# Six small reorderings in a two-block transformer kernel: a DVE scalar moved, buffers added and moved, priorities raised, the key tile before the query tile

## The chip, the cores and the metric

The kernel runs on one core of a Trainium2 chip. The time is device time of one execution in microseconds (us). PE is the matrix engine (TensorE), PEld its weight loads, DVE the vector engine, ACT the scalar engine, POOL is GpSimd, and SP issues most of the DMAs.

## The reference

Two transformer blocks on 512 tokens of width 1024, in float32.

```
first block:   mods = silu(c) @ w_mod + b_mod            (shift, scale, gate; for c and for c_ctx)
               px = (rms(x)*g*(1+sc1)+sh1) @ w_in         (the same for 256 context tokens)
               og = gated linear attention, both ways;  od = differential attention
               x  = x + gt1 * (concat(og, od) @ w_out)
               x  = x + gt2 * swiglu(rms(x)*g*(1+sc2)+sh2)
second block:  x  = x + rms(mixer(rms(x)))                (pooling, and forget-gate attention, 8 heads)
               x  = x + rms(memory_attention(rms(x), mem))(4 heads, 256 memory tokens)
               x  = x + rms(conv_ffn(rms(x)))
```

## The kernel before, in words

Activations lie feature-major: 8 tiles of 128 features by 512 tokens. Each float32 product is made of three matmuls: a matrix is split into a high part (rounded by ACT, line 187) and a low part (a subtraction, line 188), and lines 196 to 198 multiply high by high, low by high and high by low. A weight block of 128 by 1024 comes by DMA into one of two `wf` buffers and is split into one of three `whi`/`wlo` pairs (`wsplit`), or into a buffer that the caller lends (`keep`). `fm` runs over output tiles `m` and, for each, over the 8 (or 22) input tiles `k`; with `HALVES` it does all its `m` for the first 256 tokens and then for the second 256. In a fixed number of places per tile it calls `step()`, which takes one step of a generator in `between`: that is how a norm of the stage before is spread over the matmuls of the next one.

The instruction order of each engine is laid out at compile time. Every instruction gets the running number `tc.cur_priority`; of the instructions that are ready in the planner's own clock, the one with the lowest number goes first. `wsplit` lowers the number by `WO` = 50 for its two split instructions. `tc.issue_after(ins)` places what is traced inside it behind `ins` on its engine. At run time each engine takes its instructions in that order and waits at each for what it needs.

Places that the change touches:

- **Start** (lines 424 to 445). `normed_x` squares the 8 tiles of x in pairs: ACT squares the even one (line 432), DVE the odd one (433) and adds both (434), PE sums over the 128 features (313, four matmuls a pair). The pair's tile `t` (tag `sqt0`) has two buffers, `u` (tag `sqt1`) one. `WU` matmuls on the identity (line 488) run on PE before the first sum. Then come the first two blocks of `w_mod` (line 353), the reciprocal root (165 to 170), the modulation and the first projection.
- **`gd`** (line 1171), one DVE instruction on a 128 by 1 column of `cols`; its only reader is `diff_merge`, hundreds of us later.
- **End of the first mixer** (line 1343): three accumulators of `w_out` that were filled ahead are added into X by DVE; the next PSUM tiles take their banks. Then `norm2` for the second half of the tokens is spread over the first `w_ffn_in` tiles: after `W4` steps its sum over features runs on PE, after three more its reciprocal root is broadcast.
- **Forget-gate attention** (lines 1569 to 1601). `fox_in(m)` makes a query and a key tile for two heads. `ev_q` takes one DVE product, two ACT casts and two DVE subtractions; `ev_k` one DVE product, six ACT copies and two DVE subtractions. `fox(hp_)` needs both for its scores (1614, 1615).
- **Memory attention** (lines 1686 to 1770). The pool `xp` holds `KV` (keys and values, 8 KB a partition), `Ym` and lent weight buffers. In the second half of the tokens, `KV` is reused as `Y` in `post` (lines 1438, 1452, 1453), whose generator `after` is stepped by the tiles of `w_up`. The heads' softmax is stepped by `head_step`; after the last `w_xq` tile a loop runs the heads left to their end. Pool `hq` lives on to the end of the kernel; `xp` is closed ahead of the second FFN, whose pool `fp2` takes its place in SBUF and holds the split weights `Fhi`/`Flo` lent to the fourth to sixth `w_up` block, the tiles `z` and `early`, and the FFN's hidden tiles.

Of the kernel before, what the change touches and what calls it, by code (L numbers as in the profile page):

```python
# [10 lines left out]
F32 = mybir.dt.float32  # L11
# [3 lines left out]
ALU = mybir.AluOpType  # L15
# [4 lines left out]
KT = D // 128  # L20
S = 512
TT = S // 128
CTX = 256
MEM = 256
# [22 lines left out]
QP = (0,)  # L47
Q3 = 0
MG = 1
WU, WX, WW = 15, 1, 5  # L50
MV, W0 = (0, 1), 1
XG = 9
ML = 0
W4, W5 = 1, 1
W1, W2 = 2, 2
X2 = (0, 2, 4)
XR, DR = (1, 3, 5, 7), (1, 3, 5, 7)
# [3 lines left out]
WO = 50  # L61
# [19 lines left out]
def kernel(ctx: ExitStack, tc: tile.TileContext, a: dict, out: bass.AP, stop=None):  # L81
    nc = tc.nc
    V, G, A, T = nc.vector, nc.gpsimd, nc.scalar, nc.tensor

    def f32(ap):
        return ap.bitcast(F32)
# [20 lines left out]
    def mis(dt=F32):  # L107
        return ps.tile([128, 512], dt, tag="mis", name="mis")
# [18 lines left out]
    def col(name, i):  # L127
        o = COLS[name][0] + i
        return cols[:, o:o + 1]
# [85 lines left out]
    def drain():  # L215
        while between:
            step()
# [171 lines left out]
    with tc.tile_pool(name="st", bufs=1) as st, tc.tile_pool(name="st2", bufs=2) as st2:  # L389
# [37 lines left out]
        def normed_x(x):  # L427

            pt = mis()
            for k in range(0, KT, 2):  # L430
                t, u = (st2.tile([128, S], F32, tag=f"sqt{j}", name="sqt", bufs=2 - j) for j in range(2))
                A.activation(t, x[:, k], AF.Square)
                V.tensor_tensor(u, x[:, k + 1], x[:, k + 1], ALU.mult)
                V.tensor_tensor(u, u, t, ALU.add)
                with tc.issue_after(warm(WU if k == 0 else WX)):
                    last_warm[0] = sum_sq(pt, u, k == 0, k == KT - 2)
            yield
            rb = st.tile([128, S], F32, tag="rbx", name="rbx")
            yield bcast(rb, rms(st, pt, TT, "x"))
            for k in range(KT):  # L440
                V.tensor_tensor(x[:, k], x[:, k], rb, ALU.mult)
                if k == 1:
                    yield
            yield
# [55 lines left out]
        hid = hidden(0)  # L500
# [667 lines left out]
        mnl = mlo[:, 4:8].rearrange("p k (u t) -> p (k u) t", u=2)  # L1168

    gd = midp.tile([128, 1], F32, name="gd")  # L1170
    V.tensor_scalar(gd, col("diff_norm_g", 0), 0.8, None, ALU.mult)

    def mem_in(k):
        m = ap2.tile([128, MEM], F32, tag="mk", name="mk")
# [116 lines left out]
    sp = ctx.enter_context(tc.tile_pool(name="sp", bufs=2))  # L1291
# [31 lines left out]
    def norm2(x, y):  # L1323
        for _ in range(W4 if x else W5):
            yield
        r = fm_stats(sp, sqs[:, x:y], "n2")
        for _ in range(3 if x else 1):
            yield
        bcast(rb[:, x:y], r)
        for k in range(KT):  # L1330
            if k % 2:
                yield
            t = sp.tile([128, S // 2], F32, tag="n2t", name="n2t")
            V.tensor_tensor(t, X[k][:, x:y], rb[:, x:y], ALU.mult)
            modulated(t, h2[0][:, k, x:y], h2[1][:, k, x:y], sc2[:, k:k + 1], mods[:, 24 + k, 0:1], sp, "n2u")

    with tc.tile_pool(name="wo", bufs=1) as wo:
        keep = kept(wo, (0, 1, -1, -1, -1), 0)
        have = {(m, 0): wsplit(a["w_out"][m].rearrange("p k m -> p (k m)"), 1024, None, keep()) for m in (3, 4)}
        for m, (p, whi, wlo) in enumerate(parts):  # L1340
            mm3(p, whi[:, 896:1024], wlo[:, 896:1024], mhi[:, 7], mlo[:, 7], False, True)
        for m, (p, _, _) in enumerate(parts):
            V.scalar_tensor_tensor(X[m], p, mods[:, 16 + m, 0:1], X[m], ALU.mult, ALU.add)
        for m in range(len(parts)):
            add_sq(X[m], m, 0, S)
        fm(a["w_out"], range(3, KT), KT, lambda k: mhi[:, k], lambda k: mlo[:, k], accs, ev_out, HALVES, after=norm2,
           keep=keep, have=have)
# [86 lines left out]
    def post(Y, gname, nextg, g2, tails, spread):  # L1434


        def ev(m, x, y, p):
            V.tensor_scalar(Y(m // 2 * 2, x, y)[:, m % 2], p, col(gname, m), None, ALU.mult)
            add_sq(p, m, x, y)

        def after(x, y):
            rbp = sp.tile([128, S // 2], F32, tag="rbp", name="rbp")
            r = fm_stats(sp, sqs[:, x:y], "post")
            yield
            bcast(rbp, r)
            yield
            rb2 = rbp.rearrange("p (o t) -> p o t", o=1).to_broadcast([128, 2, S // 2])
            held = hq.tile([128, 2, S // 2], F32, tag="hld", name="hld")
            for k in range(0, KT + 2, 2):
                if k < KT:  # L1450
                    y2, x2 = Y(k, x, y), XT[k // 4][:, k % 4:k % 4 + 2, x:y]
                    V.tensor_tensor(y2, y2, rb2, ALU.mult)
                    V.tensor_tensor(x2, x2, y2, ALU.add)
                    for j in (k, k + 1):
                        A.activation(g2[0][:, j, x:y], X[j][:, x:y], AF.Copy, scale=col(nextg, j))
                    t = held if k == 0 else sp.tile([128, 2, S // 2], F32, tag="sqx", name="sqx", bufs=1)
                    A.activation(t, x2, AF.Square)
                    yield
                if k > 0:
                    for j in (k - 2, k - 1):  # L1460
                        V.scalar_tensor_tensor(g2[1][:, j, x:y], X[j][:, x:y], col(nextg, j), f32(g2[0][:, j, x:y]),
                                               ALU.mult, ALU.subtract)
                    if k > 2:
                        V.tensor_tensor(held, held, last, ALU.add)
                    yield
                if k < KT:
                    last = t

            def tail():
                pt = sums()  # L1470
                for j in range(2):
                    sum_sq(pt, held[:, j], j == 0, j == 1)
                r = rms(sp, pt, (y - x) // 128, "pre")
                if spread:
                    bcast(rb[:, x:y], r)
                return r
            tails[x] = tail
        return ev, after
# [12 lines left out]
    bhi, blo = (lambda k: g2[0][:, k]), (lambda k: g2[1][:, k])  # L1491
# [78 lines left out]
    def fox_in(m):  # L1570


        qs, ka = qkF[:, m % 2, 0], qkF[:, m % 2, 1]
        kl = fpl.tile([128, 2, S], F32R, tag="kl", name="kl", bufs=2)

        def scaled(p):
            t = ft.tile([128, 16 + S], F32, tag="u", name="qk")[:, :S]
            V.tensor_tensor(t, p, rb, ALU.mult)
            return t

        def ev_q(_, x, y, p):
            t = scaled(p)
            for e in range(2):
                own, oth = slice(64 * e, 64 * e + 64), slice(64 - 64 * e, 128 - 64 * e)
                A.copy(qs[own, e], t[own])
                V.tensor_tensor(qs[oth, e], t[own], f32(qs[own, e]), ALU.subtract)

        def ev_k(_, x, y, p):
            t = scaled(p)
            for e in range(2):  # L1590
                own, oth = slice(64 * e, 64 * e + 64), slice(64 - 64 * e, 128 - 64 * e)
                A.copy(ka[own, e], t[own])
                V.tensor_tensor(kl[own, e], t[own], f32(ka[own, e]), ALU.subtract)
                A.copy(ka[oth, e], t[own])
                A.copy(kl[oth, e], f32(kl[own, e]))
        fm(a["w_q2"], [m], KT, bhi, blo, accs, ev_q)
        fm(a["w_k2"], [m], KT, bhi, blo, accs, ev_k)
        return qs, ka, kl
    fox_ops = [fox_in(0)]

# [81 lines left out]
    hq = ctx.enter_context(tc.tile_pool(name="hq", bufs=1))  # L1682
    xa = ExitStack()
    xp = xa.enter_context(tc.tile_pool(name="xp", bufs=1))
    xt = xa.enter_context(tc.tile_pool(name="xt", bufs=2))
    KV = xp.tile([128, 8, MEM], F32, name="KV")
    KVM, VM = KV[:, 0:4], KV[:, 4:8].rearrange("p (t u) n -> p t (u n)", t=2)
    g4 = new_q()
    Ym = xp.tile([128, KT, S], F32, name="Ym")
# [5 lines left out]
    if stop == "x3":  # L1695
        return finish()
    nc.sync.dma_start(KV, kvd)
    xh = hp.tile([128, 8, S], F32R, tag="hhi", name="xh")
# [52 lines left out]
    def head_step(i):  # L1751
        if next(heads[i], heads) is heads:
            heads.pop(i)
# [5 lines left out]
    for i, seg in enumerate(HALVES):  # L1759
        fm(a["w_xq"], range(4), KT, lambda k: g4[0][:, k], lambda k: g4[1][:, k], accs, head_in, (seg,), keep=xk, have=wq,  # L1760
           every=XE, lo_eng=LQ and G)
        while heads:
            for i in range(len(heads))[::-1]:
                head_step(i)
        fm(a["w_xo"], range(KT), 4, lambda k: xh[:, k], lambda k: xh[:, 4 + k], accs, ev, (seg,),
           keep=lambda: room.pop(0) if room else ok(), have=wo, every=2, lo_eng=LO and G)
        drain()
        between.append(after(*seg))
# [5 lines left out]
    bhi, blo = (lambda k: g4[0][:, k]), (lambda k: g4[1][:, k])  # L1774
# [197 lines left out]
```

## Time and profile before

| | us |
|---|---|
| median of three runs | 1642.4 (1641.32 to 1644.54) |
| the profiled execution, its time | 1641.52 |
| its span (first to last instruction) | 1639.1 |
| PE busy within the span | 1590.6 (97%) |
| DVE, ACT, POOL busy | 948.0, 718.7, 214.1 |

The granted TensorE clock is 0.989 of full speed over the span. The profiled execution has 2.4 us outside its span.

### The profile page before, as it was taken

What the parts mean: (1) busy time and instruction counts of PE and PEld (TensorE: products, weight loads), DVE (VectorE), ACT (ScalarE), POOL (GpSimd) and SP (SyncE); (2) the same over time, 40 slices, a digit from 0 to 9 for tenths busy, and PEclk for the clock granted to TensorE, in tenths of its full rate; (3) what the DMA queues carried; (4) which work ended last, traced back from release to release, by engine and by line L of the source; (5) the groups of instructions that cost most, each with busy time, mean ns of one, the idle gap of its engine ahead of it and who ended that gap; (6) DMA issues with size and microseconds to landing.
All of it is one profiled execution on the core that took longest, in us unless ns stands there. A gap on an engine that the chain in (4) does not pass through costs nothing.

```text
span 1639.1 us, 25459 instructions
## 1 busy us (share of the span) xinstructions
PE 1590.6 (97%) x10098; PEld 1355.6 (83%) x10098; DVE 948.0 (58%) x1791; ACT 718.7 (44%) x1353; POOL 214.1 (13%) x237
## 2 busy tenths in 40 slices
PE   7999999999999999999999999999998999999997
PEld 5798977778889888888889777888988988888887
DVE  5626898788765222223335676445788777776333
ACT  3424555677645323232223565224466544444221
POOL 0300000111022122210004000122000222221001
PEclk8999999999999999999999999999999999999999
DMA  8232245332322333333332212234211233323332
GB/s 350 82 89 78 66 158 180 124 100 78 128 88 78 103 94 99 91 99 94 93 114 72 77 39 65 91 103 148 84 52 34 83 93 100 103 90 97 97 93 74
DMA packets 49046, 163.23 MB, mean 100 GB/s; under 512 B 5664, under 2 KB 11296, under 8 KB 47392
## 3 DMA queue, kind: packets, MB, share of 16 engines
q1 hardware_dynamic: 45328, 158.15, 30.4%
q10 hardware_dynamic: 3312, 3.18, 0.6%
q8 instruction: 79, 1.29, 0.3%
q0 software_dynamic: 288, 0.28, 0.1%
q14 instruction: 39, 0.32, 0.1%
HBM read 158.72 MB, written 3.15 MB: 99 GB/s over the span
## 4 chain that ended last, share of the span: by engine, by line
PE 85%; DVE 5%; ACT 3%; DMA 1%; issue 1%; POOL 0%; ACTq 0%; DVEq 0%; POOLq 0%
PE acc L197 16%; PE acc L198 16%; PE acc L196 16%; PE s L198 5%; PE s L196 5%; PE s L197 5%; PE acc L286 3%; PE acc L285 3%; PE acc L287 3%; PE mis L1147 1%; PE mis L1632 1%; DVE wlo L188 1%; PE acc L775 1%; PE s L1118 1%; DMA mk<-in_memT 1%
## 5 line engine op out<-in xcount | busy, mean ns | idle before, releaser
L187 ACT CAST whi<-wf 128x1024 fp32r<-128x1024 f32 (+4 forms) x221 | 228.6, 1034 | 422.6 <-PE acc L197 277.7
L188 DVE TENSOR_TENSOR wlo<-wf,whi 128x1024 fp32r<-128x1024 f32 (+2 forms) x183 | 222.0, 1213 | 176.2 <-ACT whi L187 172.3
L196 PE MATMUL acc<-qhi,whi 128*128 128x512 f32 (+1 forms) x640 | 239.4, 374 | 0.0
L197 PE MATMUL acc<-qlo,whi 128*128 128x512 f32 (+1 forms) x640 | 239.3, 374 | 0.0
L198 PE MATMUL acc<-qhi,wlo 128*128 128x512 f32 (+1 forms) x640 | 239.3, 374 | 0.0
L196 PEld LDWEIGHTS acc<-qhi,whi 128*128 128x128 f32 x640 | 120.8, 189 | 19.6
L197 PEld LDWEIGHTS acc<-qlo,whi 128*128 128x128 f32 x640 | 120.7, 189 | 19.7 <-issue 0.2
L198 PEld LDWEIGHTS acc<-qhi,wlo 128*128 128x128 f32 x640 | 120.7, 189 | 19.3
L196 PE MATMUL s<-qhi,whi 128*128 128x512 f32 (+1 forms) x336 | 128.3, 382 | 0.0
L198 PE MATMUL s<-qhi,wlo 128*128 128x512 f32 (+1 forms) x336 | 128.3, 382 | 0.0
L197 PE MATMUL s<-qlo,whi 128*128 128x512 f32 (+1 forms) x336 | 128.2, 382 | 0.0
L188 POOL TENSOR_TENSOR wlo<-wf,whi 128x1024 fp32r<-128x1024 f32 x38 | 91.0, 2396 | 214.3 <-ACT whi L187 214.3
L1417 DVE TENSOR_TENSOR e<-e,s 128x512 f32<-128x512 f32 (+1 forms) x22 | 14.3, 651 | 154.2 <-PE s L198 154.1
L197 PE MATMUL acc<-glo,whi 128*128 128x512 f32 (+1 forms) x208 | 74.4, 358 | 0.1
L196 PE MATMUL acc<-ghi,whi 128*128 128x512 f32 (+1 forms) x208 | 74.4, 358 | 0.0
L198 PE MATMUL acc<-ghi,wlo 128*128 128x512 f32 (+1 forms) x208 | 74.2, 357 | 0.0
L196 PEld LDWEIGHTS s<-qhi,whi 128*128 128x128 f32 x336 | 64.0, 190 | 11.9
L197 PEld LDWEIGHTS s<-qlo,whi 128*128 128x128 f32 x336 | 64.0, 190 | 11.8
L198 PEld LDWEIGHTS s<-qhi,wlo 128*128 128x128 f32 x336 | 63.9, 190 | 11.8
L197 PE MATMUL acc<-Flo,whi 128*128 128x512 f32 (+1 forms) x187 | 71.6, 383 | 0.0
L285 PE MATMUL acc<-whi,hhi 128*128 128x256 f32 (+1 forms) x224 | 67.1, 299 | 3.4 <-ACT qsq L654 2.5
L286 PE MATMUL acc<-wlo,hhi 128*128 128x256 f32 (+1 forms) x224 | 65.6, 293 | 3.3 <-DVE wlo L188 3.3
(648 smaller groups left out, 3833.4 us busy)
## 6 DMA issues: line engine op xcount, KB each, us to landing
wf<-in_w_ffn_in SPq DMA_DIRECT2D x44, 512.0 KB, 3.6
wf<-in_w_up SPq DMA_DIRECT2D x44, 512.0 KB, 3.5
wm<-in_w_mod SPq DMA_DIRECT2D x32, 512.0 KB, 3.6
wm<-in_w_mod SPq DMA_DIRECT2D x8, 1024.0 KB, 11.7
wf<-in_w_ffn_out SPq DMA_DIRECT2D x16, 512.0 KB, 3.5
wf<-in_w_g SPq DMA_DIRECT2D x16, 512.0 KB, 3.5
wf<-in_w_down SPq DMA_DIRECT2D x16, 512.0 KB, 3.5
wf<-in_w_dv SPq DMA_DIRECT2D x8, 512.0 KB, 3.7
```

The source lines that it names most:

```text
L187: A.copy(hi[:, :n], wf[:, :n])
L188: (lo_eng or V).tensor_tensor(lo[:, :n], wf[:, :n], f32(hi[:, :n]), ALU.subtract)
L196: T.matmul(o, lhi, rhi, start=start, stop=False)
L197: T.matmul(o, lhi, rlo, start=False, stop=False)
L198: ins = T.matmul(o, llo, rhi, start=False, stop=stop).ins
L285: T.matmul(o, bhi(k), whi, start=k == 0, stop=False)
L286: T.matmul(o, bhi(k), wlo, start=False, stop=False)
L287: T.matmul(o, blo(k), whi, start=False, stop=k == KT - 1)
L775: T.matmul(p[32 * j:32 * j + 32, :256], silc[:, 4 * kc + j], wf[:, j * 256:(j + 1) * 256], start=kc == 0, stop=kc == 1, skip_group_check=T ...
L1118: T.matmul(s_[:, n0:n1], QF[:, c, ts], KA[:, c, n0:n1], start=True, stop=False)
L1147: T.matmul(p[:, :128], aT[:, kt * 128:(kt + 1) * 128], v, start=kt == 0, stop=kt == NKT - 1)
L1632: T.matmul(pO[:, ts], vz[:, kt, hp_, 64 * e:64 * e + 128], pT[:, kt * 128:(kt + 1) * 128], start=kt + e == 0, stop=kt - t + e == 1, skip_g ...
```

## The change

1. `WU`, the identity matmuls ahead of the first sum, goes from 15 to 13, and `u` in `normed_x` gets a second buffer.
2. `gd` is issued behind `hid`, the last DVE instruction of the first modulation.
3. `norm2` for the second half takes two steps before its sum over features (`W4`) and two after it, where it took one and three.
4. The three additions of line 1343 get a number lower by 100.
5. The broadcast tile `rbp` of `post` shares the tag `n2t` of the same shape; `KV` moves from pool `xp` to pool `hq`.
6. `fox_in` makes the key tile first, then the query tile.
7. The loop that finishes the last heads of memory attention gets numbers lower by 100.

```diff
-WU, WX, WW = 15, 1, 5
+WU, WX, WW = 13, 1, 5
-W4, W5 = 1, 1
+W4, W5 = 2, 1
...
-                t, u = (st2.tile([128, S], F32, tag=f"sqt{j}", name="sqt", bufs=2 - j) for j in range(2))
+                t, u = (st2.tile([128, S], F32, tag=f"sqt{j}", name="sqt", bufs=2) for j in range(2))
...
-    V.tensor_scalar(gd, col("diff_norm_g", 0), 0.8, None, ALU.mult)
+    with tc.issue_after(hid):
+        V.tensor_scalar(gd, col("diff_norm_g", 0), 0.8, None, ALU.mult)
...
-        for _ in range(3 if x else 1):
+        for _ in range(2 if x else 1):
             yield
...
+            tc.cur_priority -= 2 * WO
             V.scalar_tensor_tensor(X[m], p, mods[:, 16 + m, 0:1], X[m], ALU.mult, ALU.add)
+            tc.cur_priority += 2 * WO
...
-            rbp = sp.tile([128, S // 2], F32, tag="rbp", name="rbp")
+            rbp = sp.tile([128, S // 2], F32, tag="n2t", name="rbp")
...
+        fm(a["w_k2"], [m], KT, bhi, blo, accs, ev_k)
         fm(a["w_q2"], [m], KT, bhi, blo, accs, ev_q)
-        fm(a["w_k2"], [m], KT, bhi, blo, accs, ev_k)
...
-    KV = xp.tile([128, 8, MEM], F32, name="KV")
+    KV = hq.tile([128, 8, MEM], F32, name="KV")
...
+        tc.cur_priority -= 2 * WO
         while heads:
             for i in range(len(heads))[::-1]:
                 head_step(i)
+        tc.cur_priority += 2 * WO
```

## Rows read from the trace of the kernel before

**Rows 1.** The page, busy time, share of the span and instructions of PE.

```profile
PE 1590.6 (97%) x10098; PEld 1355.6 (83%) x10098; DVE 948.0 (58%) x1791; ACT 718.7 (44%) x1353; POOL 214.1 (13%) x237
```

**Rows 2.** Windows: stretch, length, busy PE PEld DVE ACT POOL (count), PEclk, DMA, GB/s.

```profile
7.00:20.00 13.00, 8.13 (x53) 6.93 (x56) 4.60 (x10) 1.73 (x4) 0.00 (x0) 0.72 1.02 413
451.50:454.50 3.00, 1.12 (x7) 0.69 (x6) 2.36 (x3) 2.09 (x3) 0.00 (x0) 1.00 0.35 86
486.00:490.46 4.46, 2.28 (x20) 2.10 (x19) 2.88 (x6) 2.18 (x5) 0.04 (x1) 1.00 0.50 151
490.46:493.87 3.41, 3.41 (x18) 3.41 (x17) 1.70 (x4) 2.61 (x5) 0.00 (x0) 0.50 0.46 133
911.00:920.00 9.00, 6.96 (x32) 5.25 (x31) 5.52 (x10) 6.79 (x11) 0.00 (x0) 1.00 0.34 113
1202.00:1210.00 8.00, 6.08 (x38) 5.03 (x37) 7.79 (x22) 6.43 (x19) 0.00 (x0) 1.00 0.01 2
1262.00:1266.84 4.84, 0.34 (x4) 0.15 (x3) 4.79 (x12) 3.51 (x8) 0.33 (x4) 0.84 0.00 0
1266.84:1272.11 5.27, 4.81 (x21) 4.51 (x22) 5.27 (x10) 5.24 (x9) 2.02 (x4) 0.50 0.41 109
1272.11:1284.11 12.00, 12.00 (x102) 12.00 (x102) 9.96 (x21) 5.59 (x11) 2.97 (x7) 1.00 0.26 85
```

**Rows 3.** Timeline of DVE, start of the kernel: start, length, operation, idle before.

```profile
6.06 0.68 DVE L434 TENSOR_TENSOR sqt<-sqt 128x512 f32<-128x512 f32 x1
...
9.40 0.15 DVE L1171 TENSOR_SCALAR gd<-cols 128x1 f32<-128x1 f32 x1 [2.52 <-DMA cols<-in_cols]
...
15.66 0.69 DVE L433 TENSOR_TENSOR sqt<-X 128x512 f32<-128x512 f32 x1 [2.01 <-PE mis L313]
16.46 0.69 DVE L434 TENSOR_TENSOR sqt<-sqt 128x512 f32<-128x512 f32 x1
```

**Rows 4.** Timeline of ACT, start: the third and fourth square.

```profile
7.74 0.63 ACT L432 ACTIVATE sqt<-X 128x512 f32<-128x512 f32 x1 [0.79 <-DMA X<-in_xT]
11.03 0.63 ACT L432 ACTIVATE sqt<-X 128x512 f32<-128x512 f32 x1 [2.66 <-DVE sqt L434]
```

**Rows 5.** Timeline of PE, start: first and last sum, second block of w_mod.

```profile
7.17 0.98 PE L313 MATMUL mis<-ones,sqt 128*128 128x32 f32 x8
...
17.20 1.92 PE L313 MATMUL mis<-ones,sqt 128*128 128x32 f32 x8 [1.00 <-DVE sqt L434]
...
23.13 1.07 PE L353 MATMUL acc<-wm,silc 128*32 128x256 f32 x16
```

**Rows 6.** Timeline of DVE, end of the first mixer.

```profile
452.13 1.23 DVE L188 TENSOR_TENSOR wlo<-wf,whi 128x1024 fp32r<-128x1024 f32 x1 [2.92 <-ACT whi L187]
453.27 0.75 DVE L1343 SCALAR_TENSOR_TENSOR X<-acc,mods,X 128x512 f32<-128x512 f32 x1
```

**Rows 7.** Timeline of DVE, entry of the first FFN.

```profile
487.57 1.23 DVE L188 TENSOR_TENSOR wlo<-wf,whi 128x1024 fp32r<-128x1024 f32 x1 [0.34 <-ACT whi L187]
488.71 0.42 DVE L1312 TENSOR_TENSOR sqs<-sqs,sqt 128x256 f32<-128x256 f32 x1
```

**Rows 8.** Timeline of PE, first scores of forget-gate attention.

```profile
919.15 0.33 PE L1615 MATMUL s<-kl,qkF 128*128 128x128 f32 x1 [1.03 <-ACT kl L1595]
```

**Rows 9.** Timeline of DVE and of PE, last heads of memory attention.

```profile
1202.44 0.69 DVE L1453 TENSOR_TENSOR X<-X,Ym 128x512 f32<-128x512 f32 x1
...
1203.91 0.44 PE L1732 MATMUL mis<-ident,sm 128*128 128x128 f32 x2 [1.14 <-DVE sm L1723]
```

**Rows 10.** Timelines of DVE, POOL and PE, entry of the second FFN.

```profile
1265.01 0.69 DVE L1453 TENSOR_TENSOR X<-X,KV 128x512 f32<-128x512 f32 x1
...
1265.90 0.13 POOL L1787 MEMSET z<- 128x2 f32 x2 [128.62 <-DVE X L1453]
...
1266.50 1.58 POOL L1792 COPY zl<-z 128x2 f32<-128x2 f32 x2 [0.47 <-DVE z L1790]
...
1266.84 0.58 PE L196 MATMUL s<-qhi,Fhi 128*128 128x256 f32 x1 [4.50 <-ACT Fhi L187]
```

## The prediction

> **What bounds the kernel now.** I read the page first. PE is busy 97% of the span [rows 1]: 1590.6 of 1639.1 us. The change takes no matmul away but two on the identity, so what it can win lies in the 48 us in which PE is not busy, and in stretches where PE is busy at half clock. I looked for every stop of PE in its timeline, then for its releaser, then cut windows around those that an edit touches. The six windows show PE short of work for 4.87, 1.88, 2.18, 2.04, 1.92 and 4.50 us (length less busy time) [rows 2]. Three of these stretches hold or are followed by a lower clock: 0.72 in the first, and 0.50 for 3.41 us from 490.46 and for 5.27 us from 1266.84; from 1272.11 the clock is 1.00 again [rows 2]. In the last window 102 matmuls take 12.00 us, 0.118 us each; by that the 18 matmuls from 490.46 would take 2.12 and lose 1.29 us to the clock, and the 21 from 1266.84 would take 2.48 of 4.81 and lose 2.33 [rows 2]. So a stop at these two places costs about half as much again, behind it, as it shows itself. I lay no rule on when the clock falls: I only count that where the stop goes, the low stretch right behind it probably goes too.
>
> **The change part by part.** Each edit is set against its own stop.
>
> *Start: `gd`, `u`, `WU`.* DVE adds the first pair at 6.06, and its next piece of work is held 2.52 us, until 9.40, by `gd`, which waits for the DMA of `cols`; nobody needs `gd` for hundreds of us [rows 3]. Meanwhile ACT squared the third pair at 7.74, when its x landed [rows 4]. Later DVE waits 2.01 us, until 15.66, for PE's sum, because `u` has one buffer [rows 3], and ACT waits 2.66 us for DVE to free `t` [rows 4]. With `gd` behind `hid` and two `u`, a pair costs DVE L433 and L434: 0.69+0.69 and some issue, about 1.5 us [rows 3]. The x transfers are 0.52 MB a pair; at 413 GB/s [rows 2] one takes 1.27 us, so the fourth is there about 7.74+1.27 = 9.0, ahead of DVE. From 6.9 three pairs take DVE to 11.4, and the last sum starts there and not at 17.20: 5.8 us earlier [rows 5]. That sum took 1.92 us where the first took 0.98 [rows 5]; the 0.94 between may go, but PE still pauses between the sums, so I take half: 5.8+0.5 = 6.3. Lower bound: only the two named waits go, 2.52+2.01 = 4.5. Upper: all of the 0.94, and as much as 1.07 more for the first block of `w_mod`, if that ran at half clock: 7.8. Would DMA take it back? The second block of `w_mod` is used at 23.13 [rows 5], then at 16.8. Behind the third pair's landing there are 0.52 of x, 0.15 of `cols` and 2.1 MB of two blocks, 2.8 MB or 6.7 us at 413 GB/s: 14.5. It lies 2.3 us clear. The two fewer identity matmuls are 0.2 us of filler ahead of a sum that waits for DVE: 0; without that cover, 0.2 won, as each is near 0.1 us by the 0.118 above. `gd` costs DVE its 0.15 us behind `hid`, beside PE's matmuls.
>
> *X additions ahead (line 1343).* PE stands 1.88 of 3.00 us [rows 2], while DVE does a 1.23 us weight subtraction first and the first addition only at 453.27 [rows 6]. The PSUM banks come free with the additions. Put ahead, the addition starts up to 1.1 us earlier, but then the subtraction is late by up to three additions of 0.75, and PE waits for that too. 0.6 (0 to 1.1).
>
> *`W4` = 2.* PE stops 2.18 us ahead of the sum of squares [rows 2], because DVE's last addition to it starts at 488.71, behind a 1.23 us weight subtraction [rows 7]. One step later means a share of a tile's matmuls in front, about 12, 1.4 us by 0.118. It covers most of the stop. At stake are 2.18+1.29 = 3.47. What is late next: the reciprocal root has one step fewer before its broadcast, and PE comes to that about when it is ready. I leave 0.65 of stop and 0.5 there: 2.3 (0.5 to 3.5).
>
> *Key before query.* PE stands 2.04 of 9.00 us; the last of it are 1.03 before the first scores, for ACT's `kl` [rows 2, 8]. `ev_k` has six copies, `ev_q` two casts; with the key tile first the six lie under the query tile's matmuls. What is late next is `ev_q`'s product, casts and subtractions, shorter but there. 1.2 (0 to 2.0). The order of loads turns with it; the DMA share of 0.34 [rows 2] leaves room.
>
> *Last heads' steps ahead.* PE stands 1.92 of 8.00 us, 1.14 at one softmax product; DVE is busy 7.79 of the 8.00 and spends 0.69 us a tile on `post`'s additions of the layer before, in front of the softmax [rows 2, 9]. Numbers lower by 100 turn these two round; the additions are needed only later. As DVE has just 0.2 us free, work is only pushed on: 1.2 (0 to 1.9).
>
> *`KV` in `hq`.* `Fhi` and `z` lie where `KV` lay. The last reader of `KV`, a 0.69 us addition, runs at 1265.01; the `z` memset, whose idle engine had waited for it, at 1265.90; `Fhi`'s first matmul at 1266.84 after 4.50 us of waiting [rows 10]. With `KV` outside the reused space, the split of `Fhi` and the memset wait for no reader of it, and the weights have their loads early. At stake: 4.50, 0.46 more of 5.27 less 4.81, and 2.33 of clock, 7.3 in all [rows 2]. But DVE is busy 4.79 of 4.84 before and 5.27 of 5.27 behind [rows 2], and what PE needs after the three lent blocks comes from the same DVE: the X tiles, their low parts, `z`. I expect one small stop of 0.5 us and a little low clock: 6.0. Lower bound: the 4.50 us only is exchanged for another wait of about 2 on DVE: 2.5. `rbp` sharing a tag: 0, as the tag's other tiles are `norm2`'s, read long before; without that, a wait of `post` for one 0.4 us addition [rows 7].
>
> Sum of the savings: 6.3+0.6+2.3+1.2+1.2+6.0 = 17.6; lower bounds 7.5, upper 23.6. The profiled execution took 1641.52 [the table above], so 1641.5-17.6 = 1623.9; it is 0.9 below the median of 1642.4, so a median of 1624 to 1625. I say 1624.
>
> **The rivals.** 0.2%, 3.3 us, is about what a measurement of this kernel can tell from no change.
>
> (1) *DVE becomes the bound at the second FFN's entry, and part of the start is given back* (0.25). For it: the full DVE rows above. Against: in the 12 us behind, DVE is busy 9.96 [rows 2], so it recovers. Then `KV` gives 2.5 and the start, where PE runs into the reciprocal root and DMA instead, 5: 17.6-3.5-1.3 = 12.8, 1628.7. [...]
>
> (2) *More than forecast* (0.12). A stop that goes also keeps the clock up behind it and every bound lies near its upper end: start 7.5, `KV` 7.2, the rest 6.5: 21.2, 1620.3 or lower to 1618.
>
> (3) *The numbers don't do what they say* (0.10). The planner's order is made anew; the edits that lower numbers, and `W4`, win nothing as the planner places the same instructions first anyway: additions, `W4`, key and heads 0, and new small stops of 3: 6.3+6.0-3 = 9.3, 1632.2; up to 1637.
>
> (4) *Slower: the ring of split weights gets late* (0.05). There are three `whi`/`wlo` pairs and 1.23 us of DVE for each low part [rows 6, 7]. If the new order lays other DVE work in front of the subtractions throughout, PE waits at each block. A block of eight input tiles serves 24 matmuls in each half of the tokens, so PE's 10098 [rows 1] are at most 210 blocks: 17.6/210 = 0.084 us a block eats the whole gain, from 0.10 a block it is slower by over 0.2%, and at 0.15 it is 1641.5-17.6+31.5 = 1655.4. Against: PE is busy 97%, so subtractions have been ahead of it elsewhere, and no edit touches the inner loops but by number.
>
> **How the numbers follow.** Forecast 0.48, with its own range 1621 to 1627. Rivals (1) 0.25, (2) 0.12, (3) 0.10, (4) 0.05. From 1618 to 1633 I hold the forecast, (1), (2) but for its tail, and half of (3). Faster by over 0.2% (below 1639.1): all but (4) and a tail of (3): 0.93. Within: 0.03. Slower: 0.04.
>
> **What would show it.** `gd` behind `hid`, the last sum of squares of x starting near 11.4, and the second `w_mod` block near 17; no wait of 4.50 at `Fhi`, and clock 1.00 in the window behind it; the stop ahead of the first FFN's sum below 1 us with full clock; no wait for `kl` at the first scores, though perhaps one for the query; softmax products without 1.14. PE's busy time should fall by 4 to 5 us, the half-clock stretches, and the rest come out of its stops. The prediction is wrong if the stops come again a few us later for the next late operand, above all at the entry of the second FFN, or if new stops stand in the inner loops, where no edit was made.

## The result and the profile after

The changed kernel takes 1625.69 us, median of 4 runs (1623.72 to 1626.96), against 1643.06 of before beside it: ratio 0.9893, 95% interval 0.9877 to 0.9908, or 17.4 us less. The forecast was 1624, with 1618 to 1633 around it. The profiled execution took 1626.83 with a span of 1625.0, so the two traces stand 14.1 us of span apart [rows 1, and the table above them]. A ratio can differ a little from the quotient of the two medians beside it.

The sum came out; most of its terms did not. Below stand the page's row for PE, then the windows that answer to those of [rows 2] (stretch, length, busy time of PE, PEld, DVE, ACT and POOL with their counts, PEclk, DMA share, GB/s):

```profile
PE 1585.2 (98%) x10094; PEld 1350.0 (83%) x10094; DVE 949.5 (58%) x1791; ACT 718.1 (44%) x1354; POOL 211.3 (13%) x237
```

```profile
7.00:20.00 13.00, 11.35 (x80) 8.48 (x80) 6.05 (x17) 3.31 (x7) 0.00 (x0) 0.74 1.01 410
...
443.50:446.10 2.60, 0.72 (x5) 0.29 (x3) 1.89 (x2) 1.01 (x2) 0.00 (x0) 1.00 0.31 128
446.27:449.69 3.42, 3.42 (x17) 3.42 (x17) 2.52 (x3) 2.22 (x4) 0.00 (x0) 0.50 0.63 200
479.50:483.24 3.74, 2.46 (x22) 2.29 (x20) 2.72 (x5) 2.47 (x4) 0.00 (x0) 1.00 0.48 142
...
1194.00:1202.00 8.00, 6.08 (x39) 5.02 (x37) 7.78 (x22) 6.44 (x19) 0.00 (x0) 1.00 0.01 2
1250.00:1262.00 12.00, 12.00 (x100) 11.84 (x100) 10.28 (x24) 9.53 (x19) 1.85 (x5) 1.00 0.20 67
```

PE is full at the second FFN's entry at clock 1.00. At the start it stops 1.65 of 13 us where it stopped 4.87. At the additions (443.50) the stop is still 1.88, and in this execution half clock (PEclk 0.50, from 446.27) follows it, which it did not in the one of before. At the last heads (1194) PE and DVE are busy as long as before, to 0.01 us: 6.08 and 7.78 of 8.00.

PE's timeline shows the same places. Behind the additions there are three stops that before did not have (at 934.59, 982.81 and 1185.69), and one that takes the place of `Fhi`'s (1280.62):

```profile
12.63 1.61 PE L313 MATMUL mis<-ones,sqt 128*128 128x32 f32 x8
...
22.47 0.50 PE L196 MATMUL s<-hhi,whi 128*128 128x512 f32 x1 [0.86 <-ACT hhi L381]
...
122.65 0.35 PE L285 MATMUL acc<-whi,hc 128*128 128x256 f32 x1 [0.97 <-DVE v_qk L166]
...
446.10 0.39 PE L196 MATMUL acc<-mhi,kh 128*128 128x256 f32 x1 [1.88 <-DVE X L1345]
...
907.14 0.33 PE L1617 MATMUL s<-qkF 128*128 128x128 f32 x1 [0.80 <-DVE qkF L1589]
...
934.59 0.38 PE L1617 MATMUL s<-qkF 128*128 128x256 f32 x1 [0.46 <-DVE sm L1622]
...
982.81 0.39 PE L1617 MATMUL s<-qkF 128*128 128x256 f32 x1 [0.46 <-DVE sm L1622]
...
1185.69 0.70 PE L1714 MATMUL s<-KV,xq 128*128 128x256 f32 x2 [1.15 <-ACT sm L1721]
...
1196.02 0.44 PE L1735 MATMUL mis<-ident,sm 128*128 128x128 f32 x2 [1.13 <-DVE sm L1726]
...
1280.62 0.50 PE L196 MATMUL acc<-qhi,whi 128*128 128x512 f32 x1 [1.42 <-DVE z L1795]
```

The start of one instruction, taken in both traces, tells how far the changed kernel is ahead, and the difference of two neighbours what a stretch gave. Each trace is one execution; how far such stretches differ between executions is told further below.

| instruction | before | after | ahead | the stretch gave |
|---|---|---|---|---|
| PE, first product of the first projection | 26.60 | 22.47 | 4.1 | 4.1 |
| PE, first product with `hc` behind `v_qk` | 132.29 | 122.65 | 9.6 | 5.5 |
| PE, product behind the additions | 454.16 | 446.10 | 8.1 | -1.6 |
| DVE, `crow`, ahead of forget-gate attention | 905.07 | 896.10 | 9.0 | 0.9 |
| PE, softmax product of the last heads | 1203.91 | 1196.02 | 7.9 | -1.1 |
| PE, `r_post` at the end | 1631.08 | 1616.75 | 14.3 | 6.4 |

So the forecast 6.3 of the start is 9.6, of which more than half comes long after the start; where the four middle edits were to give 5.3, the kernel gives back 1.8 (-1.6, 0.9, -1.1); and `KV`'s 6.0 is 6.4.

### The profile page after: what moved, and what is told of

It is laid out like the page before. It is cut to its first block, busy times and chain, and to the rows that moved or that the text cites. A ratio compares the mean times of both kernels' runs of the same rounds, so it can differ in the third digit from the quotient of the medians.

```text
span 1625.0 us, 25446 instructions
## 1 busy us (share of the span) xinstructions
PE 1585.2 (98%) x10094; PEld 1350.0 (83%) x10094; DVE 949.5 (58%) x1791; ACT 718.1 (44%) x1354; POOL 211.3 (13%) x237
## 4 chain that ended last, share of the span: by engine, by line
PE 85%; DVE 6%; ACT 4%; DMA 3%; issue 2%; POOL 1%; SPq 0%; ACTq 0%; DVEq 0%; POOLq 0%
PE acc L197 16%; PE acc L196 16%; PE acc L198 16%; PE s L196 5%; PE s L198 5%; PE s L197 5%; PE acc L285 2%; PE acc L286 2%; PE acc L287 2%; PE mis L1635 1%; PE mis L1147 1%; DVE wlo L188 1%; ACT whi L187 1%; PE acc L775 1%; PE s L1118 1%
## 5 line engine op out<-in xcount | busy, mean ns | idle before, releaser
L187 ACT CAST whi<-wf 128x1024 fp32r<-128x1024 f32 (+4 forms) x221 | 228.6, 1034 | 420.8 <-PE acc L197 281.9
L1420 DVE TENSOR_TENSOR e<-e,s 128x512 f32<-128x512 f32 (+1 forms) x22 | 14.3, 651 | 154.0 <-PE s L198 153.8
```

The source lines that it names most:

```text
L187: A.copy(hi[:, :n], wf[:, :n])
```

## The experiments

Each builds on the kernel before, unless it says otherwise.

### The start, edit by edit

The whole start edit (13 identity matmuls, two `u`, `gd` behind `hid`):

> Before with the whole start edit (13 identity matmuls, two u, gd behind hid) and nothing else. In the profile of the changed kernel PE starts the first projection 4.1 us earlier, at 22.47, and reaches the first product of the linear attention (L285, 132.29 before) 9.6 us earlier: the stop of 2.90 us at 67.47 and the half clock behind it are gone as well. If the start edit does all of that alone, this run shows the same and is 8 to 10 us faster. The prediction's reading (6.3 us, all of it within the first 24 us) would leave the stop at 67 us where it was. The rival that another edit removes that stop gives 4 to 6 us.

1634.13 against 1644.16 us, ratio 0.9949 (0.9932 to 0.9966). The start's edits do it alone: 8.4 us by the ratio, 10 by the medians.

Only the count:

```diff
-WU, WX, WW = 15, 1, 5
+WU, WX, WW = 13, 1, 5
```

> Before with 13 in place of 15 identity matmuls and nothing else. The prediction counted this at 0 to 0.2 us: the time stays within 0.5 us of before and the stop at 67.47 stays. The rival: the count also enters the clock in which the order is laid out, the matmuls from 50 to 75 us come in another order, and with it the stop of 2.90 us and the half clock behind it go: 3 to 5 us faster, with the stops of the first 20 us as before (2.60, 1.28, 1.00).

1643.48, ratio 1.0004 (0.9992 to 1.0016). The rival falls: the laid-out order does change in some places between 50 and 75 us, but the stop there stays (2.77 us, with half clock behind it).

Only `gd`:

```diff
-    V.tensor_scalar(gd, col("diff_norm_g", 0), 0.8, None, ALU.mult)
+    with tc.issue_after(hid): V.tensor_scalar(gd, col("diff_norm_g", 0), 0.8, None, ALU.mult)
```

> Before with gd behind hid and nothing else. The prediction: the 2.52 us wait of DVE goes, the second sum starts near 8.9 in place of 11.05, and the later wait for the one u buffer stays: 2 to 2.5 us faster. Rival: the single u holds the pairs back just as long, so that all the gain needs both edits: under 0.7 us. A third way: with less idle time in the first 20 us the clock of the sums rises too, and it is 3 to 4 us.

1641.87, ratio 0.9987 (0.9975 to 1.0000): 2.1 us by the ratio, which is the forecast's figure, but the interval runs from 0 to 4.1 and doesn't rule out the rival. In the trace PE starts the first projection at 25.55, 1.05 us earlier than before. DVE's timeline says why it is less than the 2.52 us that `gd` held:

```profile
8.41 0.69 DVE L433 TENSOR_TENSOR sqt<-X 128x512 f32<-128x512 f32 x1 [1.03 <-PE mis L313]
...
11.06 0.69 DVE L433 TENSOR_TENSOR sqt<-X 128x512 f32<-128x512 f32 x1 [1.17 <-PE mis L313]
...
14.56 0.69 DVE L433 TENSOR_TENSOR sqt<-X 128x512 f32<-128x512 f32 x1 [2.01 <-PE mis L313]
```

The 2.52 us of `gd` [rows 3] are gone, and each later pair now waits for PE's sum of the pair before, 1.03, 1.17 and 2.01 us, 4.2 in all. The first of these waits, 1.03, was hidden behind `gd`'s; the other two stood in the kernel before as well.

Only the second `u`:

```diff
-                t, u = (st2.tile([128, S], F32, tag=f"sqt{j}", name="sqt", bufs=2 - j) for j in range(2))
+                t, u = (st2.tile([128, S], F32, tag=f"sqt{j}", name="sqt", bufs=2) for j in range(2))
```

> Before with a second buffer for u and nothing else; gd still stands in front of the second pair until the DMA of cols has landed. The prediction counts the wait of 2.01 us for PE's sum as gone: about 2 us faster, with the stop of 2.60 us ahead of the second sum unchanged. Rival: gd alone sets the chain, and this gives under 0.7 us.

1633.39, ratio 0.9937 (0.9921 to 0.9954): some 10 us, five times the forecast, and as much as the whole start edit. In its DVE timeline two things differ from before:

```profile
7.57 0.69 DVE L434 TENSOR_TENSOR sqt<-sqt 128x512 f32<-128x512 f32 x1
...
9.73 0.15 DVE L1171 TENSOR_SCALAR gd<-cols 128x1 f32<-128x1 f32 x1 [1.33 <-DMA cols<-in_cols]
9.81 1.29 DVE L433 TENSOR_TENSOR sqt<-X 128x512 f32<-128x512 f32 x2
11.02 1.29 DVE L434 TENSOR_TENSOR sqt<-sqt 128x512 f32<-128x512 f32 x2
...
56.11 1.29 DVE L188 TENSOR_TENSOR wlo<-wf,whi 128x1088 fp32r<-128x1088 f32 x1 [0.71 <-ACT whi L187]
57.32 3.17 DVE L424 TENSOR_TENSOR cX<-cX,rbc 128x256 f32<-128x256 f32 x8
```

With two `u`, the second pair is laid out ahead of `gd`. `gd` still holds the third pair for 1.33 us, but then two pairs go through together, and PE starts the first projection at 22.80, 3.8 us earlier than before:

```profile
22.80 0.49 PE L196 MATMUL s<-hhi,whi 128*128 128x512 f32 x1 [0.86 <-ACT hhi L381]
```

And 45 us later the second low part of `w_gv` (56.11) stands ahead of the context's eight products. In the kernel before it stands behind them and behind the eight subtractions that take turns with POOL, and PE stands for it, with half clock after. DVE, PE and the window behind, of before:

```profile
68.70 0.43 DVE L383 TENSOR_TENSOR hc<-mc,hc 128x256 fp32r<-128x256 f32 x1 [0.38 <-POOL mc L382]
69.04 1.28 DVE L188 TENSOR_TENSOR wlo<-wf,whi 128x1088 fp32r<-128x1088 f32 x1
```

```profile
70.38 0.41 PE L286 MATMUL acc<-wlo,hhi 128*128 128x272 f32 x1 [2.90 <-DVE wlo L188]
```

```profile
70.62:74.03 3.41, 3.41 (x17) 3.41 (x17) 2.54 (x6) 2.12 (x5) 0.00 (x0) 0.50 0.51 163
```

To tell this order from the start itself, one run moves the split and leaves `u` single:

```diff
-        affine(scc, "norm1_g", 8, 1)
+        affine(scc, "norm1_g", 8, 1); get = tm_load(a["w_gv"], 0, 272)
         for k in range(KT):
             modulated(cX[:, k], ...
...
-    get = tm_load(a["w_gv"], 0, 272)
     for t in range(2, 6):
```

> Before with one thing moved: the first w_gv block's loads and splits are written ahead of the modulation of the context tokens, so that DVE makes the second low part ahead of the context's eight products and not behind its last eight subtractions. u has one buffer as before, and the stops of the first 20 us are to stay. Theory: the second u won about 4.6 us not at the start but by turning this order; then the stop of 2.90 us before L286 and the half clock behind it (1.7 us) go, and this run is 4 to 4.6 us faster. The rival: the stop went because PE came to it at another time, and with the order alone turned PE stops at the same place for the context's rows instead: under 1 us.

1639.13 against 1644.01, ratio 0.9970 (0.9957 to 0.9983), 4.9 us. DVE makes the low part between the products, and PE's window has no stop and full clock:

```profile
60.49 2.64 DVE L424 TENSOR_TENSOR cX<-cX,rbc 128x256 f32<-128x256 f32 x7 [1.21 <-ACT rbc L333]
63.05 1.48 DVE L188 TENSOR_TENSOR wlo<-wf,whi 128x1088 fp32r<-128x1088 f32 x1
```

```profile
66.00:74.00 8.00, 8.00 (x66) 8.00 (x65) 6.66 (x14) 4.58 (x11) 3.70 (x5) 1.00 0.26 92
```

From the start of the first projection to the first product with `hc` behind `v_qk` it is 99.6 us in this trace, 99.5 to 100.8 in the six traces with two `u`, and 102.9 to 105.8 in the seven others. So the order gives the second stretch by itself; by time it is about half of the second `u`'s gain.

### The other edits, one at a time

`KV` in `hq`, with the shared tag of `rbp`:

> Before with KV in pool hq, and rbp sharing the tag n2t, and nothing else. The prediction: 6.0 us faster (2.5 to 7.3): no wait of 4.50 us at Fhi, no half clock behind it, one small stop of about 0.5 us left. Its rival: DVE is the bound there and PE stops at z or at the low parts instead, 2.5 us faster.

1636.57 against 1643.78, ratio 0.9955 (0.9939 to 0.9970), 7.4 us. There is no wait at `Fhi`, and a stop of 1.41 us at `z` some 26 us on, as in the whole change:

```profile
1293.13 0.50 PE L196 MATMUL acc<-qhi,whi 128*128 128x512 f32 x1 [1.41 <-DVE z L1790]
```

`W4 = 2`, with two steps behind the sum:

> Before with two steps ahead of the sum of squares and two behind it, and nothing else. The prediction: 2.3 us faster, the stop of 2.18 us down to 0.65 and 0.5 left in front of the broadcast or in the clock. The profile of the changed kernel shows a stop of 1.28 there, none at the broadcast and no half clock, which would be 0.90 + 1.29 = 2.2. A rival: the half clock behind the stop stays, and it is 0.9.

1642.24, ratio 0.9994 (0.9980 to 1.0007): not to be told from no change by time. In its trace the stop ahead of the sum is 1.39 us, with no half clock behind it.

The key tile first:

> Before with the key tile ahead of the query tile and nothing else. The prediction: 1.2 us faster, the three stops of 2.04 us around the first scores falling to 0.8. A rival, from the profile of the changed kernel: it is this edit that brings new stops of 0.46 us at the later scores (934 and 982 us) and one of 1.15 us in memory attention (1184.55, where the split of a late weight stands ahead of a softmax on ACT); then it gives 0 or loses up to 1 us.

1643.39, ratio 0.9997 (0.9984 to 1.0009). The three stops of 2.04 us around the first scores become one of 0.79 (at 918.87), and two of 0.45 and 0.46 us come at later scores (946.29 and 994.51). The stop at 1185.69 does not come with it, so that part of the rival falls.

The lower numbers on the additions:

> Before with the lower numbers on the three additions of line 1343 and nothing else. The prediction: 0.6 us faster, the stop of 1.88 us down to 1.3. The rival, by the profile of the changed kernel, where the weight subtraction still stands ahead of the addition that PE waits for: 0, within 0.5 us, and the stop stays 1.88. Apart from that the first mixer may lose up to 1.7 us where the half clock follows the same stop.

1644.29, ratio 0.9994 (0.9979 to 1.0008). DVE's timeline:

```profile
451.91 0.74 DVE L1343 SCALAR_TENSOR_TENSOR X<-acc,mods,X 128x512 f32<-128x512 f32 x1
452.57 1.22 DVE L188 TENSOR_TENSOR kl<-wf,kh 128x1024 fp32r<-128x1024 f32 x1
456.64 1.23 DVE L188 TENSOR_TENSOR wlo<-wf,whi 128x1024 fp32r<-128x1024 f32 x1 [2.85 <-ACT whi L187]
457.78 0.74 DVE L1343 SCALAR_TENSOR_TENSOR X<-acc,mods,X 128x512 f32<-128x512 f32 x1
```

The number moved another addition, ahead of a `kl`. The one for which PE stands still comes behind the `wlo`, as in [rows 6].

The heads' numbers, laid out alone, give the same instructions in the same order on all five engines, and so does the whole change without them. The edit is worth nothing by construction; it was not run alone.

### Two edits, three, and one more

The second `u` and `KV` (with `rbp`) only:

> Before with the second u and KV in hq (with the shared tag of rbp), and nothing else. If those two carry the change, the sum of their own runs, 10.4 + 7.4 = 17.8 us, comes out here, ratio near 0.989, as for the whole change. The rival: the other edits (13 identity matmuls, gd, W4, the additions, the key tile, the heads) give about 3 us together, as the prediction had it (0.6 + 2.3 + 1.2 + 1.2 and part of the start); then this is 14 to 15 us faster, ratio 0.991.

1626.85 against 1644.01, ratio 0.9897 (0.9883 to 0.9912), 17 us: these two carry the change. The product of their own ratios is 0.9937 x 0.9955 = 0.9892.

`W4` on top of them:

> As the run with u and KV, and W4 = 2 as well. W4's trace alone showed the stop falling from 2.18 to 1.39 us without the half clock behind it, 2.1 us, while its time moved by 1.0 us within an interval of over 2. If the trace tells the truth, this is 1 to 2 us below the run without it. The rival: the clock falls behind another stop instead, and the two are equal.

1624.49, ratio 0.9882 (0.9865 to 0.9898). The intervals overlap, the traces differ. First PE and the window behind the sum without `W4`, then with it:

```profile
479.58 0.60 PE L313 MATMUL mis<-ones,sqs 128*128 128x32 f32 x4 [2.25 <-DVE sqs L1312]
```

```profile
480.87:484.28 3.41, 3.41 (x18) 3.41 (x18) 1.70 (x4) 2.52 (x5) 0.00 (x0) 0.50 0.53 150
```

```profile
483.49 0.60 PE L313 MATMUL mis<-ones,sqs 128*128 128x32 f32 x4 [0.77 <-DVE sqs L1312]
```

```profile
448.27:451.68 3.41, 3.41 (x19) 3.41 (x18) 1.69 (x4) 1.04 (x1) 0.00 (x0) 0.50 0.77 235
...
483.49:486.90 3.41, 3.41 (x28) 3.35 (x29) 2.35 (x7) 2.07 (x6) 0.00 (x0) 1.00 0.59 171
```

The earlier window of the run with `W4` (448.27) has half clock behind the stop at the additions, without an edit there; the run without `W4` has it too (from 443.32). At the sum, the stop falls by 1.48 us, and 3.41 us now hold 28 matmuls in place of 18, 10 x 0.118 = 1.2 us: 2.7 together.

That pair of traces is a favourable one: of the ten traces with one step ahead of the sum six show half clock behind it and four do not, and the stop is 1.73 to 2.56 us; in the four with two steps it is 0.77 to 1.39 and half clock never follows. From the product behind the additions to the softmax of the last heads it is 748.4 and 748.9 us in the two traces with `W4` and no edit to the additions, the key tile or the heads, and 749.3 to 751.9, in the mean 750.7, in the nine with one step and the query tile first: about 2 us.

Last, the weight subtraction placed behind the addition that PE waits for, on top of `u`, `KV` and `W4`:

```diff
-        (lo_eng or V).tensor_tensor(lo[:, :n], wf[:, :n], f32(hi[:, :n]), ALU.subtract)
+        with tc.issue_after(add_at.pop()) if add_at else ExitStack(): (lo_eng or V).tensor_tensor(lo[:, :n], wf[:, :n], f32(hi[:, :n]), ALU.subtract)
...
-            V.scalar_tensor_tensor(X[m], p, mods[:, 16 + m, 0:1], X[m], ALU.mult, ALU.add)
+            add_ins = V.scalar_tensor_tensor(X[m], p, mods[:, 16 + m, 0:1], X[m], ALU.mult, ALU.add).ins
+            if m == 1: add_at.append(add_ins)
```

> As the run with u, KV and W4, and the weight subtraction at the end of the first mixer placed behind the addition that PE waits for (line 1343), which the lower number did not bring about. The addition then starts when PE's last product is out, and the stop of 1.88 us falls to 0.9 to 1.0: 0.9 us faster than the run without it, up to 2.5 if the half clock behind the stop goes too. The rival: the subtraction is now the late one and PE stops for it a few us later by as much; equal.

1623.86, ratio 0.9878 (0.9864 to 0.9892). PE's timeline, and the window behind the stop:

```profile
223.69 0.65 PE L775 MATMUL acc<-wm,silc 128*32 128x256 f32 x4 [2.18 <-DMA wm<-in_w_mod]
...
447.05 0.36 PE L196 MATMUL acc<-mhi,kh 128*128 128x256 f32 x1 [0.94 <-DVE X L1343]
```

```profile
447.05:450.40 3.35, 3.35 (x28) 3.35 (x29) 2.90 (x4) 1.92 (x3) 0.00 (x0) 1.00 0.39 97
```

DVE's timeline shows that the addition now starts as soon as PE's last product is out:

```profile
446.15 0.75 DVE L1343 SCALAR_TENSOR_TENSOR X<-acc,mods,X 128x512 f32<-128x512 f32 x1 [3.12 <-PE acc L198]
```

The stop is half as long, as expected, and no half clock follows it. By time, this, the run before it and the whole change (0.9893) are not told apart.

## Why the prediction was right, point by point

- **The bound.** Right: all that was won came out of PE's stops and the half clock behind them. PE's busy time fell by 5.4 us, where 4 to 5 was forecast, and its idle time by 8.7, from 48.5 to 39.8.
- **Start: 6.3, measured 9.6 in the trace: the term is mis-sized, and its size has another cause.** Its own part was 4.1 by the first projection. Executions differ there: the first projection starts at 26.60 to 28.14 in the seven traces with the old start, of which before is the earliest, and at 20.91 to 24.22 in the six with two `u`, and the two means stand 5.1 apart. The second `w_mod` block began at 18.47, not near 17. The last sum began at 12.63, not 11.4: the step "from 6.9 three pairs take DVE to 11.4" left out that the layout puts the third pair's addition behind the fourth pair's product, and x of the fourth pair was squared only at 10.03, when it landed, not at 9.0; and the sums still ran at low clock (0.74 in the window). DVE and ACT of the changed kernel:

```profile
8.92 0.69 DVE L433 TENSOR_TENSOR sqt<-X 128x512 f32<-128x512 f32 x1
10.07 0.69 DVE L433 TENSOR_TENSOR sqt<-X 128x512 f32<-128x512 f32 x1 [0.46 <-PE mis L313]
10.68 1.29 DVE L434 TENSOR_TENSOR sqt<-sqt 128x512 f32<-128x512 f32 x2
```

```profile
10.03 0.63 ACT L432 ACTIVATE sqt<-X 128x512 f32<-128x512 f32 x1 [0.65 <-DMA X<-in_xT]
```

  The step that failed was to add up the waits that the profile names, 2.52 for `gd` and 2.01 for `u`. `gd` alone brought the first projection 1.05 us forward, since one of `u`'s waits stood hidden behind it; the second `u` alone brought it 3.8 forward, since the layout then put `gd` behind a pair, and `gd` adds nothing to that (20.91 to 24.22 without its edit, 22.47 and 23.57 with it). And the prediction stopped at the second `w_mod` block. The new layout turned an order at 56 us, worth 4.9 us by itself, which no row of the start could show. One price was wrong without consequence: an identity matmul took not 0.1 but 0.39 us (13 in 5.10, from 1.89), yet two fewer gave nothing by time, as forecast.
- **X additions: 0.6, measured 0.** The failed step is "Put ahead, the addition starts up to 1.1 us earlier": the lower number did not put it ahead. The probable reason, argued only, is that an instruction with a lower number still has to be ready in the planner's clock when DVE is free there, and this one waits for PE's last product. When the subtraction was put behind it by an explicit order, 0.94 of the stop went, close to the upper bound. The prediction priced the right thing and did not doubt that the edit does it; its third rival did.
- **`W4`: 2.3, about 2 by the traces, not shown by time.** The mechanism holds: the stop is shorter and no half clock follows it. Its sign was a stop below 1 us, and it was 1.28. The table's 0.9 for that stretch is small because the half clock behind the additions took 3.42 less 17 x 0.118, 1.4 us, there. That is no loss by an edit: of the thirteen traces with a stop of 1.76 to 2.13 us at the additions ten have half clock behind it, and the one of before is among the three without.
- **Key first: 1.2, about 0.3 in the trace** (2.04 less 0.79, 0.45 and 0.46), and not to be told from 0 by time. "What is late next is `ev_q`" was right for the first scores; the two later stops, for `sm`, were not foreseen.
- **Heads: 1.2, measured 0.** The step that failed is "Numbers lower by 100 turn these two round": the order stayed as it was, and the stop of 1.14 at the softmax product is 1.13. Again the edit was taken to do what it says.
- **`KV`: 6.0, measured 6.4 in the trace and 7.4 by time.** Right, and the firmest of all: from the softmax of the last heads to `r_post` it is 420.7 to 420.8 us in the five traces with `KV` in `hq`, and 426.8 to 428.1 in the nine without. The forecast that a small stop would come next was right in kind (1.42 us at `z`). Rival (1), DVE as the bound there, is out: in the 12 us from 1250 PE has no idle time while DVE is busy 10.28. Two low parts of `Flo` and the `z` memset (1245.73 in place of [rows 10]'s 1265.90) moved ahead of `post`'s additions into time that DVE and POOL had free:

```profile
1246.65 1.23 DVE L188 TENSOR_TENSOR Flo<-wf,Fhi 128x1024 fp32r<-128x1024 f32 x1 [0.60 <-ACT Fhi L187]
...
1248.13 1.22 DVE L188 TENSOR_TENSOR Flo<-wf,Fhi 128x1024 fp32r<-128x1024 f32 x1
```

- **POOL's copies beside DVE.** POOL's copies of one 128x2 tile took from 0.18 to 1.11 us there. The short one began where DVE stood still (1254.28 to 1254.45). The long one began 0.14 us into a DVE subtraction of 1.21 us and ended 0.04 us behind it. POOL, then DVE:

```profile
1254.34 0.18 POOL L1797 COPY zl<-z 128x2 f32<-128x2 f32 x1 [0.35 <-DVE z L1795]
...
1261.11 1.11 POOL L1797 COPY zl<-z 128x2 f32<-128x2 f32 x1 [3.15 <-DVE z L1795]
```

```profile
1260.97 1.21 DVE L188 TENSOR_TENSOR Flo<-wf,Fhi 128x1024 fp32r<-128x1024 f32 x1
```

  Two other copies, of 0.58 and 0.98 us (at 1253.41 and 1262.97), lay beside a DVE that was busy all that time too. Whether DVE held any of them up was not shown. PE lost nothing to it in that window: it is busy 12.00 of the 12.00 us from 1250.
- **The sum.** 17.6 against 17.4 us by the medians, and against 14.7 by the two profiled executions. By time the second `u` and `KV` carry 17 of it, where the start and `KV` were to give 12.3; the additions and the heads give 0 where 1.8 was forecast, and `W4` and the key tile, forecast at 3.5, are not to be told from 0 by time. That errors of both signs cancel to within 1 us is luck.

  Three losses between the two profiled executions have no edit shown behind them, and make their distance smaller than that of the medians. From `hc` to the additions (132 to 454 us before) the changed kernel is 1.6 us longer, 323.5 against 321.9, but in the eleven traces without a late `w_mod` block that stretch varies from 320.4 to 323.5. The half clock behind the additions cost 1.4. And some 1.5 went between 905 and 1204 us, mostly in the stop at 1185.69.

Left open: that last stop. ACT's split of a `w_xo` block waits 2.01 us for its DMA at 1183.77, so that the softmax behind it is late. The DMA landed 5.53 us after its issue, where it took 3.52 before. The same split waits 1.73 us in the run of the start edit (PE then stops 0.87 us) and 1.16 in the run of the count alone (PE: 0.30), and at most 0.65 in the eleven other traces, in which PE has no stop of over 0.1 us there. So the three traces with 13 identity matmuls are the three with the stop; whether the count causes it or three executions fell that way was not tested.

## What to carry to other kernels

When two waits stand one behind the other on one engine, the profile may name only the first, as it named `gd`'s 2.52 us here and not the 1.03 behind it; price them together, and try each alone. An edit of a number in a planner's order is worth nothing until the laid-out order shows that the instruction moved; an explicit "behind that one" did what the priority had not (the stop at the additions went from 1.88 to 0.94 us). And in such a kernel a buffer at the start can turn an order tens of microseconds later (here at 56 us, an order worth 4.9 us by itself): compare the order of the instructions there, before and after, before you credit the place that was edited. Last, compare a stretch between two traces only when you know how far it varies between executions without any edit (from `hc` to the additions by 3.1 us here).

## What the runs showed of the hardware that was not expected

The same stop was not always followed by half clock. The 1.88 us at the additions was followed by full clock (1.00) in the trace of before and by 3.41 us at 0.50 after the change, for a loss of about 1.4 us; over all traces, ten of thirteen such stops had it behind them. The stop of 0.94 had none, but that is one trace. And the `w_mod` load used near 230 us landed late in three of the traces: PE waited 1.71 us for it in the run of `KV`, 2.13 in the run of the additions and 2.18 in the last run, each with 6.83 us of half clock beside it, and not at all at that place in the profiled execution of before. In these three traces the stretch from `hc` to the additions is 325.2 to 327.7 us. That may be part of what keeps the runs of one kernel some 3 us apart; it was not tested.
